# A power on GpSimd in place of a logarithm, an exponential and three corrections

## The chip, the cores and the metric

The kernel runs on one core of a Trainium2 chip. Five engines work side by side, each with a queue of its own that it executes in order: TensorE (PE, matmuls; its weight loads are shown as PEld), VectorE (DVE), ScalarE (ACT), GpSimd (POOL) and SyncE (SP, which here only issues transfers). The metric is the device time of one execution in microseconds (us); lower is better.

## The reference

The reference is one layer of a streaming encoder for 528 new frames of one stream (16 learned meta tokens and 512 prompt frames) and 64 further frames of a running stream with 128 cached ones. The model width is 2048.

```python
def rmsnorm(x, g):
    y = x * lax.rsqrt(jnp.mean(x * x, axis=-1, keepdims=True) + EPS)
    return y * g

h = rmsnorm(x, norm_attn_g)
z = h @ w_in                                  # q, k, v of 8 differential heads; latents of MLA
cq = rmsnorm(z[..., OFF_CQ:OFF_CKV], mla_q_norm_g);  qm = cq @ mla_w_uq
ckv = rmsnorm(z[..., OFF_CKV:OFF_KR], mla_kv_norm_g); km, vm = expand_latent(ckv, mla_w_ukv)
o_d, o_m = attention(...)                     # chunk-causal, both head groups
o_d = rmsnorm(o_d, diff_subln_g) * (1 - lam_init)     # one norm per head of 128 columns
x = x + concatenate([o_d, o_m]) @ w_out
h = rmsnorm(x, norm_ffn_g)
x = x + (silu(h @ w_gate) * (h @ w_up)) @ w_down      # inner width 5632
y = rmsnorm(x, final_norm_g)
```

Everything is float32. The new keys, values and latents are outputs too.

## The kernel before, in words

Activations are held transposed, features on the 128 partitions and tokens along the columns: T = 592 columns with the meta tokens, TQ = 576 without. Every weight and activation is split into a high and a low part (`wh`, `wl`; `xh`, `xl`): ScalarE writes the high part with a copy to a reduced format, VectorE subtracts it from the original, and TensorE multiplies high by high, high by low and low by high.

Because tokens run along the columns, the mean square of a token is a sum over partitions. A matmul with a matrix of ones gives that sum on all 128 partitions at once, so that the reciprocal square root of a norm is taken of a whole 128x576 or 128x592 tile in most places. `rsqrt(r, v)` does this: a logarithm (`Ln`) and an exponential of minus a half of it (`Exp`) on ScalarE, and then one correction step of Newton's method on VectorE, in three instructions, the last of which writes r. `v` is overwritten.

The places are these, in order of time:

- the norm before attention: squares are summed with tokens on the partitions, so `ss` and `rc` are 128x5 only; ten small matmuls (`prb`) then spread `rc` over the columns as `rb`, with which the projections' results are scaled (`z`)
- `diff_attend`, once for each of the eight differential heads: the head's output `o32` (name `o` in the profile), its squares `sq`, the sum `pq`, the mean square written back to `sq` by VectorE, `rsqrt(r, sq)`, and the scaling of `o32` by `g08` and `r`. The outputs of heads 0 to 6 are stored to DRAM (`mspill`) and loaded back for the output projection; head 7's is split into `mxh` and `mxl` at once
- `key_latent_norm` (`v`, `r`, then `zl` scaled), whose results are transposed for an output and serve as keys and values of the second head group
- `query_norm` (`v`, `rsq`): `rsq` multiplies the projected queries of the second head group (`zq`, `zn`)
- `token_norm` before the FFN (`sq2` and `rb2`, shown as `sq` and `rb`): `rb2` multiplies the gate's sums `c` before and after SiLU, in `gated`
- `token_rows`, the last stage, with tokens on the partitions again: four groups of 128 tokens and one of 64, with a mean square of 128x1 or 64x1 each. Groups 0 to 3 call `rsqrt`. The last group has a written-out form of it, in which the logarithm takes its sum and bias itself while VectorE writes `v`.

TensorE's instructions run in the order in which the program lists them. A small model of time (`Streams`) decides in what order the generators for projections, heads and norms are advanced while the program is written, and so how matmuls of different stages interleave. VectorE's, ScalarE's and SyncE's instructions keep their written order only in the first stage, in the stretch from the last head to the start of the FFN, and where `pin` is used; elsewhere the order of their queues is set by the program builder from written order, dependencies and its own estimates of durations. GpSimd's queue is always ordered in that second way. GpSimd otherwise holds some fills (`bias`, `p`), additions of squares, parts of the rotary embedding, and in the FFN the sums of weight blocks (`ws`) and products of `c`.

The attention stage uses a PSUM bank pair `sp` (one buffer) for scores; VectorE's instruction `e<-sp,bias` adds the bias and frees it. The pair `ps` (two buffers) takes projections. Weights of the projections have two buffers each for `wh` and `wl`.

In the last stage ScalarE's table set with logarithm and exponential is loaded again by a pinned `preload_act_table_set`; SiLU in the FFN uses another set.

Of the kernel before, what the change touches and what calls it, by code (L numbers as in the profile page):

```python
# [11 lines left out]
F32 = mybir.dt.float32  # L12
F32R = mybir.dt.float32r
AF = mybir.ActivationFunctionType
ALU = mybir.AluOpType
# [4 lines left out]
P = 128  # L20
D = 2048
# [110 lines left out]
def encoder_step(  # L132
# [8 lines left out]
    V, S, Q, G = Engine(tc, nc.vector), Engine(tc, nc.scalar), Engine(tc, nc.sync), nc.gpsimd  # L141
# [3 lines left out]
    cp = ctx.enter_context(tc.tile_pool(name="cp", bufs=1))  # L145
# [7 lines left out]
    def store(dst, src):  # L153
        Q.dma_start(dst, src)
# [3 lines left out]
    def f32(ap):  # L158
        return ap.bitcast(F32)
# [8 lines left out]
    def split_scaled(hi, lo, src, g):  # L168
        S.activation(hi, src, AF.Copy, scale=g)
        V.scalar_tensor_tensor(lo, src, g, f32(hi), op0=ALU.mult, op1=ALU.subtract)  # L170

    def rsqrt(r, v):

        S.activation(r, v, AF.Ln)
        S.activation(r, r, AF.Exp, scale=-0.5)
        V.tensor_tensor(v, v, r, op=ALU.mult)
        V.scalar_tensor_tensor(v, v, -0.5, r, op0=ALU.mult, op1=ALU.mult)
        V.scalar_tensor_tensor(r, v, 1.5, r, op0=ALU.add, op1=ALU.mult)

    def weights(src, kcs, cols, pool=None):  # L180
        pool = pool or wp
# [179 lines left out]
    with ExitStack() as ph:  # L361
# [25 lines left out]
        x = {}  # L387
# [942 lines left out]
    def pin(ins):  # L1330
        if pinned[0]:
            tc.keep_in_program_order(ins)
# [37 lines left out]
    def pmt():  # L1370
        return pm.tile([P, 512], F32, name="m", tag="m")
# [117 lines left out]
    for i in range(KC):  # L1489
        x = ma.tile([P, TQ], F32, name="x", tag="x", bufs=3)  # L1490
# [352 lines left out]
    def column(i, o, n):  # L1843
        if i in columns:
            return columns[i][:, o:o + n]
        return y5[0][:, o:o + n] if o + n <= 384 else y5[1][:, o - QH:o - QH + n]

    def token_rows(g, d):

        o, n = groups[g]  # L1850
        q, last = d // 2, g == len(groups) - 1
        fine = last and d > 5
        if d % 2 == 0 or fine:
            banks0[g, q] = pmt()
        bank = banks0[g, q][0:n, :]
        c0 = d % 2 * 256
        for k, (hi, lo) in enumerate(acts):
            wh, wl = kept[d][k]
            for i, (a, b) in enumerate(((hi, wh), (hi, wl), (lo, wh))):
                PE.matmul(bank[:, c0:c0 + 256], a[:, o:o + n], b, start=k + i == 0,  # L1860
                          stop=k == len(acts) - 1 and i == 2)
        for f in range(2):
            c = c0 + f * P
            PE.matmul(bank[:, c:c + P], column(2 * d + f, o, n), ident, start=False, stop=True,  # L1864
                      is_transpose=True, skip_group_check=True)
        ss = small[0:n, 8 * g:8 * g + 8]
        v, b, r = (small[0:n, a + g:a + g + 1] for a in (40, 48, 56))
        cs = slice(c0, c0 + 256) if fine else slice(0, 512)
        if d % 2 or fine:
            at = q + (last and d == 7)  # L1870
            S.activation(junk[0:n, cs], bank[:, cs], AF.Square, accum_out=ss[:, at:at + 1])
            if last and d < 7:
                V.tensor_tensor(whole[0:n, 512 * q + cs.start:512 * q + cs.stop], bank[:, cs], gain[q][0:n, cs],
                                op=ALU.mult)
        if last and d == 6:
            V.tensor_reduce(b, ss[:, 0:4], axis=AX.X, op=ALU.add)
            V.tensor_scalar(b, b, 1.0 / D, EPS, op0=ALU.mult, op1=ALU.add)
        elif last and d == 7:
            x = ss[:, 4:5]
            S.activation(r, x, AF.Ln, bias=b, scale=1.0 / D)  # L1880
            V.scalar_tensor_tensor(v, x, 1.0 / D, b, op0=ALU.mult, op1=ALU.add)
            S.activation(r, r, AF.Exp, scale=-0.5)
            V.tensor_tensor(v, v, r, op=ALU.mult)
            V.scalar_tensor_tensor(v, v, -0.5, r, op0=ALU.mult, op1=ALU.mult)
            V.scalar_tensor_tensor(r, v, 1.5, r, op0=ALU.add, op1=ALU.mult)
            w = whole[0:n, :]
            V.scalar_tensor_tensor(w[:, 1792:2048], bank[:, cs], r, gain[3][0:n, cs], op0=ALU.mult, op1=ALU.mult)
            S.activation(w[:, 0:512], w[:, 0:512], AF.Copy, scale=r)
            V.tensor_scalar(w[:, 1024:1792], w[:, 1024:1792], r, None, op0=ALU.mult)
            store(y_sample[:, 1024:2048], w[:, 1024:2048])  # L1890
            S.activation(w[:, 512:1024], w[:, 512:1024], AF.Copy, scale=r)
            S.dma_start(y_sample[:, 0:1024], w[:, 0:1024])
        elif d == 7:
            V.tensor_reduce(v, ss[:, 0:4], axis=AX.X, op=ALU.add)
            V.tensor_scalar(v, v, 1.0 / D, EPS, op0=ALU.mult, op1=ALU.add)
            rsqrt(r, v)
            for q in range(4):
                ot = room(names)[0:n, 0:512]
                V.scalar_tensor_tensor(ot, banks0.pop((g, q))[0:n, :], r, gain[q][0:n], op0=ALU.mult, op1=ALU.mult)
                store(y_prompt[o:o + n, q * 512:(q + 1) * 512], ot)  # L1900
# [18 lines left out]
    for bi, n in enumerate(blocks):  # L1919
        slots = [(first + k) % 8 for k in range(n)]  # L1920
        if bi + 1 < len(blocks):
            if bi + 2 == len(blocks):
                build = builder(first + n, blocks[bi + 1])
            else:
                build = fetcher(first + n, 4)

            def step():
                next(start, None)
                next(build, None)
                next(keeping, None)  # L1930
                next(late, None)

            keeping, late = iter(()), iter(())
            if bi + 2 == len(blocks):
                rest = [m for m in range(8) if m not in slots]
                free = [f"b{p}_{m}" for m in rest[::-1][:2] for p in ORDER]
                free += [f"b{p}_{m}" for m in rest[:-2] for p in (3, 6, 7)]
                free += [f"b{p}_{m}" for m in slots for p in ORDER]
                names = iter(free)
                fifth_raws, fifth_weights = (itertools.cycle([next(names) for _ in range(2)]) for _ in range(2))  # L1940
            for d in range(KC // 2):
                if bi + 2 == len(blocks) and d == 2:
                    keeping = plain_weights(first + n)
                if bi + 2 == len(blocks) and d == 4:
                    S.activation(y5[0][:, QH:384], y5[1][:, 0:384 - QH], AF.Copy)
                if bi + 3 == len(blocks) and d == KC // 2 - 1:
                    late = late_parts(first + n + 4)
                if bi == 0 and d == 1:
                    accumulator(4, y234[:, 2 * TQ:3 * TQ])
                    y5 = [None, y234[:, 3 * TQ:3 * TQ + QH]]  # L1950
                    load(y5[1], x2spill[5, :, QH:TQ])
                    fetch_raw(first, n, 3)
                elif bi == 0 and d == 2:
                    Q.ordered = False
                    close_fb()
                    yy, close_yy = pool("yy")
                    y5[0] = yy.tile([P, 384], F32, name="y5")
                    y[5] = [y5[0][:, 0:QH], y5[1]]
                    load(y[5][0], x2spill[5, :, 0:QH])
                if bi == 0 and 2 < d < KC // 2 - 1:  # L1960
                    fetch_raw(first, n, d + 1)
                if bi == 0 and d > 1:
                    for i in range(2 * d + 2, min(2 * d + 4, KC)):
                        accumulator(i, yy.tile([P, TQ], F32, name=f"y{i}"))
                if (first, d) not in fetched:
                    fetch_raw(first, n, d)
                down_rows(first, n, d, slots, step)
            for g in (build, keeping, late):
                for _ in g:
                    pass  # L1970
        else:
            pin(S.preload_act_table_set("natural_log_exp_and_others"))

            small, junk = room(names), room(names)[:, 0:512]
            whole = fr.tile([P, 2048], F32, name="whole", tag="raw", bufs=2)
            gain = [room(names)[:, 0:512] for _ in range(4)]
            for q in range(4):
                load(gain[q], g_fin[q * 512:(q + 1) * 512].unsqueeze(0).to_broadcast([P, 512]))
            for g in range(5):
                for d in range(KC // 2):  # L1980
                    token_rows(g, d)
        first += n
# [78 lines left out]
```

## Time and profile before

| what | value |
|---|---|
| median of 3 runs | 2387.84 us (2387.77 to 2390.52) |
| span of the profiled execution | 2389.4 us |
| profiled execution against the median | 1.6 us above it, inside the runs' range |
| TensorE busy | 2361.4 us (99%) |
| VectorE busy | 1794.6 us (75%) |
| ScalarE busy | 1161.9 us (49%) |
| GpSimd busy | 705.5 us (30%) |
| first projections and first norm | 0 to 65 us |
| projections and differential heads | 65 to 520 us |
| latent heads and output projection | 520 to 790 us, its second part and the first FFN weights to 935 us |
| gate and up projections | to about 1860 us |
| down projection | to about 2343 us |
| last block, final norm and outputs | to 2389.4 us |

The profile's span runs from the first to the last instruction of the profiled execution; no time around it is listed. In lines of the timeline the first number is the start in us from the beginning of the span, the second the length in us, then engine, line, operation, the tile written and the tiles read, and in brackets how long the engine had been idle before and for what. Most instructions of VectorE, ScalarE and SyncE go through one helper and so have line L125; they are told apart by their tiles. In lines that group instructions, an x with a number is their count.

### The profile page before, as it was taken

What the parts mean: (1) busy time and instruction counts of PE and PEld (TensorE: products, weight loads), DVE (VectorE), ACT (ScalarE), POOL (GpSimd) and SP (SyncE); (2) the same over time, 40 slices, a digit from 0 to 9 for tenths busy, and PEclk for the clock granted to TensorE, in tenths of its full rate; (3) what the DMA queues carried; (4) which work ended last, traced back from release to release, by engine and by line L of the source; (5) the groups of instructions that cost most, each with busy time, mean ns of one, the idle gap of its engine ahead of it and who ended that gap; (6) DMA issues with size and microseconds to landing.
All of it is one profiled execution on the core that took longest, in us unless ns stands there. A gap on an engine that the chain in (4) does not pass through costs nothing.

```text
span 2389.4 us, 44637 instructions
## 1 busy us (share of the span) xinstructions
PE 2361.4 (99%) x17558; PEld 2330.0 (98%) x17558; DVE 1794.6 (75%) x2878; ACT 1161.9 (49%) x2262; POOL 705.5 (30%) x553
## 2 busy tenths in 40 slices
PE   9999999999999999999999999999999999999998
PEld 8999999999999999999999999999999999999998
DVE  5665656776555788788888888888888888888984
ACT  5544445455444554445545555545545433333444
POOL 0000000020001345554454454554554322222320
PEclk9999999999999999999999999999999999999999
DMA  9423333353223553334434434434434975645432
GB/s 277 125 85 86 93 87 94 94 157 116 89 94 107 168 176 108 120 112 151 154 118 151 155 116 151 163 110 155 160 113 153 324 260 170 227 161 169 159 102 98
DMA packets 330547, 340.93 MB, mean 143 GB/s; under 512 B 22610, under 2 KB 272376, under 8 KB 330304
## 3 DMA queue, kind: packets, MB, share of 16 engines
q1 hardware_dynamic: 328720, 334.30, 43.1%
q0 software_dynamic: 1104, 3.22, 0.4%
q8 instruction: 138, 2.26, 0.4%
q10 hardware_dynamic: 512, 0.55, 0.1%
q14 instruction: 73, 0.60, 0.1%
HBM read 267.21 MB, written 74.15 MB: 143 GB/s over the span
## 4 chain that ended last, share of the span: by engine, by line
PE 58%; DVE 1%; DMA 1%; issue 0%; POOL 0%; ACT 0%; DVEq 0%; POOLq 0%; SPq 0%; ACTq 0%
PE m L1454 38%; PE m L1458 19%; PE m L1860 1%; DVE wl L125 1%; DMA raw<-in_ffn_w_down 1%; PE m L1864 0%; DVE ws L125 0%; DMA b<-sumspill 0%; POOL ws L1414 0%; DVE y L125 0%; ACT b L125 0%; DVE b L125 0%; DVE whole L125 0%; DVE c L125 0%; ACT whole L125 0%
## 5 line engine op out<-in xcount | busy, mean ns | idle before, releaser
L1454 PE MATMUL m<-b,wh 128*128 128x288 f32 x7168 | 1052.5, 296 | 4.1 <-DVE y L125 2.7
L1454 PEld LDWEIGHTS m<-b,wh 128*128 128x128 f32 x7168 | 984.0, 189 | 6.7 <-ACT wh L125 4.2
L1458 PE MATMUL m<-b,wl 128*128 128x288 f32 x3584 | 569.8, 295 | 2.0 <-DVE wl L125 1.9
L1414 POOL TENSOR_TENSOR ws<-raw 128x512 f32<-128x512 f32 (+1 forms) x258 | 366.7, 1430 | 542.0 <-DVE wl L125 237.8
L1458 PEld LDWEIGHTS m<-b,wl 128*128 128x128 f32 x3584 | 509.2, 189 | 3.5 <-DVE wl L125 3.4
L125 ACT ACTIVATE wh<-ws 128x512 fp32r<-128x512 f32 (+1 forms) x339 | 282.9, 845 | 393.9 <-PE m L1454 244.4
L125 DVE TENSOR_TENSOR wl<-ws,wh 128x512 fp32r<-128x512 f32 (+1 forms) x339 | 386.8, 1149 | 98.5 <-ACT wh L125 93.0
L125 DVE TENSOR_TENSOR wl<-raw,wh 128x512 fp32r<-128x512 f32 (+1 forms) x393 | 367.8, 959 | 13.5 <-ACT wh L125 11.1
L125 ACT ACTIVATE wh<-raw 128x512 fp32r<-128x512 f32 (+1 forms) x393 | 230.9, 620 | 291.8 <-PE m L1454 241.6
L108 PE MATMUL ps<-xh,wh 128*128 128x296 f32 (+1 forms) x960 | 217.6, 308 | 1.7 <-ACT wh L125 1.7
L108 PE MATMUL ps<-xl,wh 128*128 128x296 f32 (+1 forms) x960 | 208.4, 298 | 0.0
L108 PE MATMUL ps<-xh,wl 128*128 128x296 f32 (+1 forms) x928 | 202.1, 299 | 0.5 <-DVE wl L125 0.5
L125 DVE TENSOR_TENSOR y<-y,m 128x288 f32<-128x288 f32 x280 | 125.4, 449 | 57.7 <-PE m L1458 56.3
L108 PEld LDWEIGHTS ps<-xh,wh 128*128 128x128 f32 x960 | 155.5, 190 | 5.5 <-ACT wh L125 2.1
L125 DVE TENSOR_TENSOR ws<-ws,raw 128x512 f32<-128x512 f32 (+1 forms) x129 | 111.7, 870 | 60.8 <-POOL ws L1414 58.5
L108 PEld LDWEIGHTS ps<-xl,wh 128*128 128x128 f32 x960 | 155.6, 189 | 0.3 <-DVE xl L125 0.2
L108 PEld LDWEIGHTS ps<-xh,wl 128*128 128x128 f32 x928 | 151.1, 189 | 1.0 <-DVE wl L125 1.0
L125 DVE TENSOR_TENSOR wl<-wr,wh 128x1024 fp32r<-128x1024 f32 (+1 forms) x106 | 111.2, 1050 | 29.8 <-ACT wh L125 28.4
L125 ACT ACTIVATE wh<-wr 128x1024 fp32r<-128x1024 f32 (+1 forms) x108 | 97.3, 903 | 59.2 <-PE ps L108 36.2
L1679 POOL TENSOR_TENSOR c<-c,rb 128x576 f32<-128x576 f32 x42 | 67.1, 1599 | 168.7 <-ACT c L125 168.7
L703 POOL MEMSET bias<- 64x64 f32 x8 | 1.2, 144 | 365.1 <-DMA bias<-tsk 311.6
L125 ACT ACTIVATE parts<-c 128x1 fp32r<-128x1 f32 (+1 forms) x266 | 85.7, 322 | 32.3 <-DVE c L125 26.3
(427 smaller groups left out, 3139.2 us busy)
## 6 DMA issues: line engine op xcount, KB each, us to landing
raw<-in_ffn_w_gate SPq DMA_DIRECT2D x44, 1024.0 KB, 5.9
raw<-in_ffn_w_up SPq DMA_DIRECT2D x44, 1024.0 KB, 6.5
raw<-in_ffn_w_down SPq DMA_DIRECT2D x39, 1024.0 KB, 5.5
partspill<-parts SPq DMA_DIRECT2D x133, 288.0 KB, 2.1
b<-partspill SPq DMA_DIRECT2D x133, 288.0 KB, 6.2
wr<-in_w_in SPq DMA_DIRECT2D x54, 512.0 KB, 3.8
wr<-in_w_out SPq DMA_DIRECT2D x16, 512.0 KB, 4.0
wr<-in_w_out SPq DMA_DIRECT2D x24, 256.0 KB, 3.0
```

The costliest lines, as they stand in the source:

```text
L108: self.tc.keep_in_program_order(self.pe.matmul(out, lhsT, rhs, start=start, stop=stop))
L125: ins = issue(*args, **kwargs)
L703: G.memset(bias[0:64, 464:528], -BIG)
L1414: engine.tensor_tensor(w[:, k:k + m, :], pick(xs), pick(ys), op=op)
L1454: PE.matmul(banks[p], wh[k], x, start=first and new and k == 0 and x is hi, stop=False, skip_group_check=not new)
L1458: PE.matmul(banks[p], wl[k], hi, start=False, stop=last and k == n - 1, skip_group_check=not new)
L1679: engine.tensor_tensor(g[:, f, :], g[:, f, :], rb2, op=ALU.mult)
L1860: PE.matmul(bank[:, c0:c0 + 256], a[:, o:o + n], b, start=k + i == 0, stop=k == len(acts) - 1 and i == 2)
```

## The change

`rsqrt` becomes one instruction on GpSimd, `r = v ** -0.5`, an elementwise power with a 128x1 tile of -0.5 spread over the columns as its second operand. That tile is filled once by VectorE at the start. All places call it; the last group of the last stage loses its written-out form and calls `rsqrt` after VectorE has written `v`. The second load of the table set with logarithm and exponential is removed.

```diff
+    minus_half = cp.tile([P, 1], F32, name="minus_half")
+    V.memset(minus_half, -0.5)
+
     def rsqrt(r, v):
-
-        S.activation(r, v, AF.Ln)
-        S.activation(r, r, AF.Exp, scale=-0.5)
-        V.tensor_tensor(v, v, r, op=ALU.mult)
-        V.scalar_tensor_tensor(v, v, -0.5, r, op0=ALU.mult, op1=ALU.mult)
-        V.scalar_tensor_tensor(r, v, 1.5, r, op0=ALU.add, op1=ALU.mult)
+        G.tensor_tensor(r, v, minus_half[0:v.shape[0]].to_broadcast(list(v.shape)), op=ALU.pow)
...
             x = ss[:, 4:5]
-            S.activation(r, x, AF.Ln, bias=b, scale=1.0 / D)
             V.scalar_tensor_tensor(v, x, 1.0 / D, b, op0=ALU.mult, op1=ALU.add)
-            S.activation(r, r, AF.Exp, scale=-0.5)
-            V.tensor_tensor(v, v, r, op=ALU.mult)
-            V.scalar_tensor_tensor(v, v, -0.5, r, op0=ALU.mult, op1=ALU.mult)
-            V.scalar_tensor_tensor(r, v, 1.5, r, op0=ALU.add, op1=ALU.mult)
+            rsqrt(r, v)
...
-            pin(S.preload_act_table_set("natural_log_exp_and_others"))
```

## The prediction

> **What bounds the kernel now.** I read the page first, its busy shares, slices and chain, then the groups of instructions on GpSimd, then the timeline around each norm.
>
> ```profile
> PE 2361.4 (99%) x17558; PEld 2330.0 (98%) x17558; DVE 1794.6 (75%) x2878; ACT 1161.9 (49%) x2262; POOL 705.5 (30%) x553
> PE 58%; DVE 1%; DMA 1%; issue 0%; POOL 0%; ACT 0%; DVEq 0%; POOLq 0%; SPq 0%; ACTq 0%
> ```
>
> The span is 2389.4 us, so TensorE is idle for 28.0 us of it, and the chain that ends last is matmuls with a per cent each of VectorE and DMA. ScalarE and VectorE work is worth nothing by itself here; it counts where it makes a matmul wait. Matmuls stand in a fixed order, so a wait is lost for good. The profiled span is 1.6 us above the median of the runs, 2387.84; I add the differences to the median. A change of 0.2% is 4.8 us, about what a measurement of this kernel can tell from none.
>
> **What is removed.** Seventeen places compute a reciprocal square root. Eleven are wide, with 576 or 592 columns (eight heads, the key latents, the query latents, the tokens before the FFN); the others are the 128x5 of the first norm, four 128x1 and the tail's 64x1. The head norms show what goes at a wide place:
>
> ```profile
> L125 ACT ACTIVATE r<-sq x8: 684/685/688, 138.5 to 509.2; 128x576 f32<-128x576 f32 x8
> L125 ACT ACTIVATE r<-r x9: 684/686/699, 139.2 to 509.9; 128x576 f32<-128x576 f32 x8, 128x592 f32<-128x592 f32 x1
> L125 DVE TENSOR_TENSOR sq<-sq,r x8: 757/759/1394, 139.9 to 510.7; 128x576 f32<-128x576 f32 x8
> L125 DVE SCALAR_TENSOR_TENSOR sq<-sq,r x8: 748/759/760, 140.7 to 512.7; 128x576 f32<-128x576 f32 x8
> L125 DVE SCALAR_TENSOR_TENSOR r<-sq,r x8: 747/758/759, 141.5 to 513.4; 128x576 f32<-128x576 f32 x8
> ```
>
> Two activations of 0.69 and three corrections of 0.76 are 3.7 us of work, about 40 us over eleven places. It lies beside matmuls and gives TensorE nothing. What matters is when the result comes.
>
> **What is added: one power per place, with no row of its own.** The nearest rows on GpSimd:
>
> ```profile
> L1796 POOL TENSOR_TENSOR c<-c 128x576 f32<-128x576 f32 x42 | 73.5, 1749 | 86.0 <-DVE c L125 82.1 <-issue 3.7
> L635 POOL MEMSET q00z<- 64x576 f32 x1 | 0.6, 583 | 50.8 <-DMA xspill<-xt 50.8
> L1414 POOL TENSOR_TENSOR ws<-b 128x128 f32<-128x128 f32 x16 | 9.8, 610 | 2.3 <-DMA b<-in_ffn_w_down 2.3
> L1353 POOL TENSOR_TENSOR b<-b 128x288 f32<-128x288 f32 x4 | 3.2, 808 | 28.5 <-ACT b L125 28.5
> ```
>
> A product of two 128x576 tiles takes 1.75 us; a pass without input takes 0.58. A power is a logarithm, a product and an exponential; ScalarE's tables do the first and last in a pass, and GpSimd shows no such pass. I count some 14 multiply-adds for the two series. Lower bound: they hide behind the reading, X = 1.75 us. Upper: each costs a full two-input pass, 15 x 1.75 = 26 us. I take each at the input-free pass, 14 x 0.58 + 1.75 = 9.9, so X = 10 us (an estimate), nearest to the memset row since a step needs no new operand. For 64x1 the two narrow rows give (808 - 610)/160 = 1.24 ns a column and so 0.45 us at none; I take 0.4, between 0 and 1.
>
> The Trainium skill's page GPSIMD Engine Reference, section on elementwise cycle accounting, says a loop body of three or more operations runs at about 3 operations a cycle at 1.2 GHz. By it 14 steps on 576 columns would be an estimated 2.2 us and the change would cost nothing (the third rival). No run here shows it.
>
> **Heads 0 to 6.** The first, on the timeline:
>
> ```profile
> 137.62 0.75 DVE L125 TENSOR_SCALAR sq<-pq 128x576 f32<-128x576 f32 x1
> 142.28 0.82 DVE L125 SCALAR_TENSOR_TENSOR o<-o,gT,r 128x576 f32<-128x576 f32 x1
> 143.19 0.77 DVE L125 TENSOR_TENSOR z<-ps,rb 128x592 f32<-128x592 f32 x1
> 146.06 0.29 DVE L125 CUSTOM_DVE_ANT_0 e<-sp,bias 128x144 f32<-128x144 f32 x1
> 147.06 0.37 PE L108 MATMUL sp<-kh,q10s 128*128 128x272 f32 x1
> ```
>
> The mean square is ready at 138.37 and the scaling of the head's output begins at 142.28. The scaling's own result is not urgent: it is stored, and read back long after. But VectorE works its queue in order, and if the scaling keeps its place, z and the score evacuation e stand behind it, and the next scores need the bank that e frees. With 0.1 us of handoff the power ends at 138.47 + 10 = 148.47; the scaling is 6.2 us late, e with it. e ended at 146.35 and the matmul began at 147.06: 0.7 us of slack. Lost: 5.5 us, generally X - 4.5. For seven heads 38.5 us. On GpSimd's queue the power has the next head's bias memset behind it, some 23 us later here, so it delays nothing there below X of about 20.
>
> **Head 7**, whose output goes straight to matmuls:
>
> ```profile
> 508.37 0.76 DVE L125 TENSOR_SCALAR sq<-pq 128x576 f32<-128x576 f32 x1
> 513.54 3.93 POOL L1009 TENSOR_TENSOR rkl<-kr,rkh 64x592 fp32r<-64x592 f32 x2 [2.11 <-ACT rkh L125]
> 514.23 1.92 DVE L125 SCALAR_TENSOR_TENSOR o<-o,gT,r 128x576 f32<-128x576 f32 x1
> 519.09 0.74 DVE L125 TENSOR_TENSOR mxl<-o,mxh 128x576 fp32r<-128x576 f32 x1
> 519.77 0.40 PE L108 MATMUL pso<-mxh,wh 128*128 128x288 f32 x1
> ```
>
> Power 509.23 to 519.23, scaling 0.82, the split's two halves 0.69 and 0.74, 0.2 between: 521.7 instead of 519.83, 1.9 us lost (X - 8.1). The scaling took 1.92 here beside GpSimd's 3.93 and 0.82 alone: the two engines slow each other. A power that computes more than it reads should do so less; I take 0, with 1.1 us for each VectorE instruction beside it as the other bound.
>
> **Key and query latents.**
>
> ```profile
> 450.10 0.77 DVE L125 TENSOR_SCALAR v<-sp 128x592 f32<-128x592 f32 x1
> 455.72 1.57 DVE L125 SCALAR_TENSOR_TENSOR zl<-zl,gT,r 128x592 f32<-128x592 f32 x2
> 458.22 0.38 PE L112 MATMUL pn<-ident,zl 128*128 128x128 f32 x2
> ...
> 528.94 0.45 DVE L125 TENSOR_SCALAR v<-pq 128x288 f32<-128x288 f32 x1
> 534.68 0.76 DVE L125 SCALAR_TENSOR_TENSOR zq<-ps,rsq 128x576 f32<-128x576 f32 x1
> 536.40 0.75 DVE L125 TENSOR_TENSOR xo<-xo,ps 128x576 f32<-128x576 f32 x1 [0.97 <-PE ps L108]
> 542.57 0.42 PE L108 MATMUL ps<-mxh,wh 128*128 128x288 f32 x2
> ```
>
> Keys: power to 460.97, two scalings to 462.6, transposes due at 458.22: 4.4 us lost (X - 5.6). Queries: power to 539.5, zq and xo to 541.1, bank due at 542.57: nothing lost (X - 11.5 above that).
>
> **Tokens before the FFN.**
>
> ```profile
> 913.34 0.81 DVE L125 TENSOR_SCALAR sq<-m 128x288 f32<-128x288 f32 x2
> 919.26 2.52 DVE L125 TENSOR_TENSOR c<-c,rb 128x576 f32<-128x576 f32 x2
> 919.42 3.51 POOL L1414 TENSOR_TENSOR ws<-raw 128x512 f32<-128x512 f32 x2 [13.55 <-DVE wl L125]
> 924.07 1.32 PE L1458 MATMUL m<-b,wl 128*128 128x288 f32 x8 [0.42 <-DVE wl L125]
> ```
>
> Power 914.25 to 924.25; the products of c start 5.0 us late, the low weight halves behind them too, and TensorE already waits for one: 5.0 us lost (X - 5). GpSimd's subtotals of 919.42, queued behind the power, are late by the same 5 us, inside that loss.
>
> **First norm and tail.**
>
> ```profile
> 59.73 0.17 DVE L125 TENSOR_SCALAR ss<-ss 128x5 f32<-128x5 f32 x1
> 60.81 0.17 DVE L125 SCALAR_TENSOR_TENSOR rc<-ss,rc 128x5 f32<-128x5 f32 x1
> 61.34 0.83 PE L108 MATMUL prb<-ident,rc 128*128 128x128 f32 x6
> ...
> 2337.33 1.28 ACT L125 ACT_TABLE_LOAD   x1
> 2381.80 0.15 DVE L125 SCALAR_TENSOR_TENSOR b<-b 64x1 f32<-64x1 f32 x1
> 2382.53 0.34 DVE L125 SCALAR_TENSOR_TENSOR b<-b 64x1 f32<-64x1 f32 x2
> ```
>
> First norm: ready at 59.90 + 0.1 + 0.4 = 60.4 instead of 60.98, the matmul busy elsewhere until 61.34: nothing. Tail: v at 2381.95, the power to 2382.45, instead of 2382.87: 0.4 us gained, and this is on the path to the end (0.8 gained to 0.2 lost). The four 128x1 places lie under matmuls of the following rows. The table load of 1.28 us leaves ScalarE among waits: nothing. The fill of minus_half stands before the first data.
>
> **Sum:** 38.5 + 1.9 + 4.4 + 0 + 5.0 - 0.4 = 49.4 us, 2387.84 + 49.4 = 2437 us. It rests on X and on the queue order.
>
> **Rivals.** *The steps run one behind the other (B).* At X = 26 the same terms are 7 x 21.5 + 17.9 + 20.4 + 14.5 + 21.0 - 0.4 = 224, giving 2612 us; for it, only that the engine's simplest wide product already takes 1.75 us where VectorE takes 0.76. The Trainium skill, same page, section on performance pitfalls, gives 4 cycles a step for a dependent chain: 14 steps would be an estimated 27 us; no run here shows it.
>
> *The queue order gives way (C).* VectorE's queue here is ordered by the program builder from its own estimates; with z, e and the FFN splits ahead of the scaling, only real readers wait: 1.9 + 4.4 - 0.4 = 5.9, 2394 us. Against it: the builder must hold the power for long.
>
> *Not slower (D).* Up to X = 4.5 the power ends no later than the old five instructions plus their slack, all terms vanish but the tail: 2387.4 us; at X = 5 it is 7 x 0.5 - 0.4 = 3.1, still within 0.2%. That X decides. For it: the lower bound of 1.75.
>
> *Faster (E).* VectorE, freed of 25 us, lets matmuls start that waited for it. It would have to end 4.8 of TensorE's 28 idle us: 2383 us. Against it: VectorE's share of the chain is 1%.
>
> **Chances:** forecast 0.36, B 0.16, C 0.09, D 0.34, E 0.05. Slower 0.61, same 0.34, faster 0.05. The forecast's own range is X of 6 to 15, 2399 to 2491 us. For 8 in 10 it goes down to 2386 (D whole) and up to X = 20, 108.5 + 11.9 + 14.4 + 8.5 + 15.0 - 0.4 = 158, 2546 us, leaving out E and most of B.
>
> **What would show it.** GpSimd's group of powers, eight of 128x576: its mean is X. Right: 7 to 13 us, VectorE's longest waits are of the scaling for r on GpSimd, and TensorE waits near the head norms and at 914 to 930. Wrong if X is below 5 (times as before, TensorE's idle time still 28), or if VectorE does other work between mean square and scaling. In the tail one GpSimd instruction should stand between v and the output, and the table load be gone.

## The result, and the profile after

The changed kernel takes 3386.39 us (median of 4 runs, 3384.77 to 3389.03), the kernel before 2387.81 us beside it (4 runs): a ratio of 1.417, with an interval of 1.415 to 1.419. It is slower, as forecast, but by 999 us where 49 were forecast. One price explains most of it. The page of the changed kernel begins:

```profile
span 3386.9 us, 44561 instructions
PE 2388.5 (71%) x17558; PEld 2353.7 (69%) x17558; DVE 1770.3 (52%) x2828; ACT 1143.7 (34%) x2227; POOL 1722.2 (51%) x570
PE   9723507154150062099995399999999999999999
PEclk9857758576675585599997699999999999999999
POOL 0376493855959948900047854445445554222231
```

GpSimd works 1722.2 us where it had 705.5. TensorE has holes in the first two fifths of the span, and in most of those slices GpSimd is busy instead and TensorE's granted clock is down. From the gate and up projections on, everything is as it was. The groups of GpSimd's instructions on `rsqrt`'s line (count, then busy time, mean ns of one) show why:

```profile
L176 POOL TENSOR_TENSOR r<-sq,minus_half 128x576 f32<-128x576 f32 x8 | 738.8, 92345 | 200.7 <-DVE sq L125 180.4 <-DMA cos<-c_cos 20.3
L176 POOL TENSOR_TENSOR r<-v,minus_half 128x592 f32<-128x592 f32 x1 | 94.8, 94757 | 7.5 <-DVE v L125 7.5
L176 POOL TENSOR_TENSOR rsq<-v,minus_half 128x576 f32<-128x576 f32 x1 | 92.2, 92194 | 2.8 <-DVE v L125 2.8
L176 POOL TENSOR_TENSOR rb<-sq,minus_half 128x576 f32<-128x576 f32 x1 | 92.6, 92601 | 8.4 <-DVE sq L125 8.4
```

One wide power takes 92.3 us, nine times the 10 us assumed and 3.5 times the 26 us of the upper bound. What TensorE waited for, from the view of the waits (us in total, times, longest):

```profile
PE pna L112 <- DVE z L125: 347.4, 4, 88.2
PE sp L108 <- DVE nm L125: 176.7, 5, 88.7
PE pn L112 <- DVE nn L125: 92.8, 1, 92.8
PE m L1452 <- ACT wh L125: 91.2, 2, 91.0
PE pn L112 <- DVE zl L125: 88.6, 2, 88.3
PE pso L108 <- ACT wh L125: 88.3, 1, 88.3
PE pso L108 <- DVE xo L125: 87.0, 1, 87.0
DVE o L125 <- POOL r L176: 738.4, 8, 92.4
```

Seven heads (4 + 2 + 1 long waits in the first three lines), the tokens before the FFN, the key latents, head 7, the query latents: eleven wide places, eleven waits of 85 to 93 us. (`pna` takes transposes of `z`; `nm` is written beside the scores' `e`; `nn` is a copy of transposed key latents. VectorE's `z`, `nm` and `nn` all stand behind a scaling in its queue.) None of these lines names GpSimd as what TensorE waited for; it is VectorE and ScalarE, and only VectorE's own wait, the last line, names the power. The first head on the timeline shows the chain:

```profile
137.72 0.75 DVE L125 TENSOR_SCALAR sq<-pq 128x576 f32<-128x576 f32 x1
138.61 92.22 POOL L176 TENSOR_TENSOR r<-sq,minus_half 128x576 f32<-128x576 f32 x1 [30.26 <-DVE sq L125]
...
230.87 0.82 DVE L125 SCALAR_TENSOR_TENSOR o<-o,gT,r 128x576 f32<-128x576 f32 x1 [92.39 <-POOL r L176]
231.60 0.77 DVE L125 TENSOR_TENSOR z<-ps,rb 128x592 f32<-128x592 f32 x1
...
232.43 1.11 PE L112 MATMUL pna<-ident,z 128*128 128x128 f32 x4 [85.42 <-DVE z L125]
```

The scaling of the head's output waits 92.39 us for r, though its own result goes only to DRAM; `z`, which does not need r, stands behind it in VectorE's queue and starts as soon as the scaling lets it; TensorE, out of work 85 us before, waits for `z`.

The sum closes. The seven lines of TensorE's waits make 972 us. TensorE is idle for 3386.9 - 2388.5 = 998.4 us, against 28.0 before: 970.4 more. It is also busy for 27.1 us more with the same 17,558 matmuls. Together 997.5, which is the difference of the spans (3386.9 - 2389.4). The 27 us come from the clock, in this table of windows around the end of the first wait (length; busy time of PE, PEld, DVE, ACT, POOL; granted clock; DMA share and GB/s):

```profile
228.00:232.40 4.40, 0.00 (x0) 0.00 (x0) 1.53 (x3) 0.00 (x0) 2.83 (x1) 0.50 0.00 0
...
236.40:238.40 2.00, 2.00 (x10) 2.00 (x9) 1.93 (x7) 0.12 (x1) 0.00 (x0) 0.50 0.06 17
238.40:240.40 2.00, 2.00 (x11) 1.94 (x10) 1.07 (x6) 1.16 (x5) 0.00 (x0) 0.54 0.47 131
240.40:242.40 2.00, 2.00 (x15) 2.00 (x14) 1.41 (x5) 0.54 (x1) 0.00 (x0) 1.00 0.08 21
```

After the wait the matmuls run at half clock until about 240, some 8 us after the first of them; ten instructions in 2 us, then fifteen. The Trainium skill's page TensorE: Matmul & The Clock Gate, Part 1, tells of two states, half clock after at least one idle window of about 3.4 us and full clock after a busy one. The trace agrees on the two states; the way back took longer here, with gaps in the first 4 us, and less idle time was enough for the fall. In the kernel before, a wait of 2.26 us ended at 1874.90, and the next 3.41 us are at half clock:

```profile
1871.76:1875.17 3.41, 1.15 (x9) 0.95 (x8) 3.41 (x8) 2.75 (x7) 1.08 (x1) 1.00 1.05 364
1875.17:1878.58 3.41, 3.41 (x16) 3.41 (x15) 2.54 (x6) 0.00 (x0) 1.70 (x3) 0.50 1.07 373
```

### The profile page after: what moved, and what is told of

It is laid out like the page before. It is cut to its first block, busy times and chain, and to the rows that moved or that the text cites. A ratio compares the mean times of both kernels' runs of the same rounds, so it can differ in the third digit from the quotient of the medians.

```text
span 3386.9 us, 44561 instructions
## 1 busy us (share of the span) xinstructions
PE 2388.5 (71%) x17558; PEld 2353.7 (69%) x17558; DVE 1770.3 (52%) x2828; ACT 1143.7 (34%) x2227; POOL 1722.2 (51%) x570
## 3 DMA queue, kind: packets, MB, share of 16 engines
q8 instruction: 138, 2.26, 0.3%
## 5 line engine op out<-in xcount | busy, mean ns | idle before, releaser
L176 POOL TENSOR_TENSOR r<-sq,minus_half 128x576 f32<-128x576 f32 x8 | 738.8, 92345 | 200.7 <-DVE sq L125 180.4
L125 DVE SCALAR_TENSOR_TENSOR o<-o,gT,r 128x576 f32<-128x576 f32 x8 | 7.7, 964 | 738.4 <-POOL r L176 738.4
L112 PE MATMUL pna<-ident,z 128*128 128x128 f32 x64 | 11.6, 313 | 347.4 <-DVE z L125 347.4
L112 PEld LDWEIGHTS pna<-ident,z 128*128 128x128 f32 x64 | 8.8, 159 | 348.4 <-DVE z L125 348.3
L125 ACT ACTIVATE kh<-z 64x592 fp32r<-64x592 f32 x32 | 22.3, 695 | 358.9 <-DVE z L125 358.5
```

Of the source, the lines that this page charges most:

```text
L112: self.tc.keep_in_program_order(self.pe.transpose(out, in_, identity))
L125: ins = issue(*args, **kwargs)
L176: G.tensor_tensor(r, v, minus_half[0:v.shape[0]].to_broadcast(list(v.shape)), op=ALU.pow)
```

## The experiments

Three groups of kernels ran on three occasions; the kernel before ran beside each, with medians of 2390.43 us (21 runs), 2390.04 (13) and 2389.92 (19), a little above the 2387.8 that the expectations use. Ratios are against the runs of the same group.

**Is it the power or the move?** A product in its place, so that queues, tiles and waits stay and only the operation differs. The power is left out.

```diff
-    V.memset(minus_half, -0.5)
+    V.memset(minus_half, 0.01)
-        G.tensor_tensor(r, v, minus_half[...].to_broadcast(...), op=ALU.pow)
+        G.tensor_tensor(r, v, minus_half[...].to_broadcast(...), op=ALU.mult)
```

> Left out: the power. The changed kernel with a product by 0.01 in its place on GpSimd, at all seventeen places; every wait, queue and order of the change stays, only the instruction is another. Theory (the price of the power, 92.2 us for 128x576, is the whole loss): the product takes about 1.6 us, less than the 4.5 us that the heads can bear, so 2387 us, within 3 us of the kernel before. Rival (moving the step to GpSimd's queue costs by itself, whatever it computes): most of the 1000 us stays, above 2600 us.

Measured: 2388.48 us (10 runs), ratio 0.9996 (0.9987 to 1.0005). The group of GpSimd's instructions at that line:

```profile
L176 POOL TENSOR_TENSOR r<-sq,minus_half 128x576 f32<-128x576 f32 x8 | 10.4, 1304 | 201.8 <-DVE sq L125 201.8
```

An operation of the same shape in the same place takes 1.3 us and costs nothing. So the whole loss comes with the power, and not with the move. It also shows that taking the activations and corrections off ScalarE and VectorE gains nothing that this can measure: VectorE is busy 1766.6 us instead of 1794.6, and the time is the same.

**Does the price go with the columns?** The power on the left half of the eleven wide places, the old five instructions (`newton`) on the rest.

```diff
     def rsqrt(r, v):
+        w = v.shape[1]
+        if w > 8:
+            newton(r[:, w // 2:w], v[:, w // 2:w])
+            r, v = r[:, 0:w // 2], v[:, 0:w // 2]
         G.tensor_tensor(r, v, minus_half[...].to_broadcast(...), op=ALU.pow)
```

> The power on the left half of the columns at the eleven wide places, the old five instructions on the right half. X should be 0.4 + 288 x 0.159 = 46.3 us, since the 128x5 power took 1.20 and the 128x576 one 92.18. Theory (VectorE waits in its queue, and the matmuls behind it, for X less a slack): 7 x (46.3 - 4.5) + 38.2 + 40.7 + 34.8 + 41.3 - 0.4 = 447 us, 2835 us, up to 25 us more where the clock sinks in the waits. Rival (GpSimd is simply too busy: a power per head has to fit the 53 us between heads): 46.3 fits, the heads lose nothing, and only head 7, the latents and the tokens cost their 155 us, 2543 us.

Measured: 2865.30 us (4 runs), ratio 1.199 (1.197 to 1.201).

```profile
L187 POOL TENSOR_TENSOR r<-sq,minus_half 128x288 f32<-128x288 f32 x8 | 370.2, 46272 | 200.2 <-DVE sq L125 200.2
```

46.3 us is half of 92.3, and the loss is halved too, with the waits (TensorE's eleven long ones are of 37.6 to 44.0 us) and 24.6 us of slower matmuls on top: the price goes by the columns, and the loss goes by the latency at each place.

**Only the narrow places.** The power at 128x5, 128x1 and 64x1, the old five at the wide ones.

```diff
     def rsqrt(r, v):
+        if v.shape[1] > 8:
+            return newton(r, v)
         G.tensor_tensor(r, v, minus_half[...].to_broadcast(...), op=ALU.pow)
```

> The power only where it is narrow (128x5, four 128x1, the tail's 64x1), the old five instructions at the eleven wide places; no second load of the table set. Theory (price by columns): the narrow ones take 0.5 to 1.2 us; the tail ends 0.4 us earlier as in the changed kernel, 2387.4 us, 0.4 us faster than before. Rival (each power has a fixed price on the engine that the first norm and the tail feel): 2389 us or more.

Measured: 2389.16 us (11 runs), ratio 0.9995 (0.9987 to 1.0004). The narrow places cost nothing. In the tail the timeline of this kernel shows

```profile
2380.96 0.19 ACT L125 ACTIVATION_READ_ACCUMULATOR b<-m 64x1 f32 x1
2381.18 0.15 DVE L125 SCALAR_TENSOR_TENSOR b<-b 64x1 f32<-64x1 f32 x1 [0.19 <-ACT b L125]
2381.41 0.54 POOL L185 TENSOR_TENSOR b<-b,minus_half 64x1 f32<-64x1 f32 x1 [6.29 <-DVE b L125]
2381.99 1.33 ACT L125 ACTIVATE whole<-whole,b 64x512 f32<-64x512 f32 x2 [0.84 <-POOL b L185]
```

From the end of the sum, 2381.15, to the output, 2381.99, are 0.84 us; before, it was 1.24. The 0.4 us are there in the trace and far below what the times can tell.

**The price by itself.** The kernel before, with nine powers of several widths, partitions, exponents and bases and one product more on GpSimd, in the first 40 us, while it has nothing to do. Nothing reads their results.

```diff
+            G.tensor_tensor(res[0:P, 0:64], lab[0:P, 0:64], lab[0:P, 96:97].to_broadcast([P, 64]), op=ALU.pow)
...
+            G.tensor_tensor(res[0:16, 96:112], lab[0:16, 0:16], lab[0:16, 96:97].to_broadcast([16, 16]), op=ALU.pow)
...
+            G.tensor_tensor(res[0:P, 192:208], lab[0:P, 0:16], lab[0:P, 98:99].to_broadcast([P, 16]), op=ALU.mult)
```

> The kernel before, with eleven extra instructions on GpSimd in its idle first 50 us, whose results nobody reads: powers of 128x64, 128x16, 64x16 and 16x16 with the exponent -0.5, of 128x16 with 0.5, 2 and 1, of the bases 1 and 0.01, and one product. Theory (a loop over columns, the same work for each): 10.6 us for 64 columns, 2.9 us for each 16, whatever the exponent and the base; 16 and 64 partitions as long as 128, if each column is done for all partitions at once. Rival (element by element within a group of partitions): with 16 partitions the same, since each of eight groups of 16 has a processor of its own. Rival (a general routine with short cuts for easy operands): exponents 1 and 2 or the base 1 take well under half. The product about 0.3 us. The time of the kernel 2388 us.

Measured: 2390.36 us in one run, and on the timeline, in the order of the code: base 1.37 with exponent -0.5 on 128x64; then on 128x16, 64x16 and 16x16; four rows of 2.88, 2.88, 2.89 and 2.89 us on 128x16, with exponents 0.5, 2 and 1 and with base 1, left out here; base 0.01; the product.

```profile
5.39 10.57 POOL L422 TENSOR_TENSOR res<-lab 128x64 f32<-128x64 f32 x1
15.93 2.89 POOL L423 TENSOR_TENSOR res<-lab 128x16 f32<-128x16 f32 x1
18.79 2.89 POOL L424 TENSOR_TENSOR res<-lab 64x16 f32<-64x16 f32 x1
21.65 2.88 POOL L425 TENSOR_TENSOR res<-lab 16x16 f32<-16x16 f32 x1
...
35.95 2.96 POOL L430 TENSOR_TENSOR res<-lab 128x16 f32<-128x16 f32 x1
38.88 0.39 POOL L431 TENSOR_TENSOR res<-lab 128x16 f32<-128x16 f32 x1
```

(10.57 - 2.89) / 48 = 0.160 us a column, and 0.33 us at none. That gives 92.5 us for 576 columns, where 92.3 were measured. Neither the partitions, nor the exponent, nor the base matter much (2.88 to 2.96): there is no short cut for a square, for a first power or for a base of one. That 16 partitions take as long as 128 fits the theory and the first rival alike; this does not tell them apart.

**The forecast's own condition.** The power on 60 columns at every wide place, so that its time is what the prediction had assumed, X = 9.9 us.

```diff
...
+        if w > 8:
+            newton(r[:, 60:w], v[:, 60:w])
+            r, v = r[:, 0:60], v[:, 0:60]
```

> The power on 60 columns at all eleven wide places, the old five instructions on the rest: X = 0.33 + 60 x 0.160 = 9.9 us, the price that the prediction assumed. Theory (the prediction's sum is right for its X): 7 x 5.4 + 1.8 + 4.3 + 0 + 4.9 - 0.4 = 48 us, 2436 us, and up to 25 us more if the clock sinks after these short waits too. Rival (short waits are taken up by idle time of VectorE behind them): under 2415 us.

Measured: 2458.44 us (4 runs), ratio 1.029 (1.027 to 1.032), or 68 us more. The power took 10.0 us. The line of the page, and below it the three largest totals among TensorE's waits (us in total, times, longest):

```profile
PE 2386.5 (97%) x17558; PEld 2352.6 (96%) x17558; DVE 1790.5 (73%) x2861; ACT 1157.2 (47%) x2249; POOL 819.7 (33%) x570
```

```profile
PE sp L108 <- DVE nm L125: 24.0, 6, 5.0
PE m L1467 <- DVE wl L125: 5.8, 3, 4.9
PE pso L108 <- ACT wh L125: 4.9, 1, 4.9
```

The waits are of 2.8 to 5.0 us at ten of the eleven places, none at the query latents, as the prediction's terms have it. TensorE is idle for 45.4 us more than before (73.4 instead of 28.0), and the terms sum to 48. That is partly luck: the seven heads lost 32 us instead of 38, head 7 lost 4.9 instead of 1.8. On top, the matmuls take 25.1 us more (2386.5 - 2361.4). So short a wait is enough to lose the clock. The windows around the first one, where TensorE is idle for 3.11 us until 150.12 and, a little later, for 1.61 until 152.38:

```profile
148.00:150.00 2.00, 0.00 (x0) 0.00 (x0) 1.44 (x3) 0.00 (x0) 0.52 (x1) 1.00 0.00 0
150.00:152.00 2.00, 0.66 (x4) 0.42 (x4) 2.00 (x4) 1.87 (x3) 0.00 (x0) 0.91 0.39 147
...
156.00:158.00 2.00, 2.00 (x10) 1.94 (x10) 1.07 (x6) 1.25 (x5) 0.00 (x0) 0.50 0.47 131
158.00:160.00 2.00, 2.00 (x14) 2.00 (x13) 1.21 (x4) 0.25 (x1) 0.00 (x0) 0.89 0.08 21
```

So even at the assumed X the forecast's 49 us would have been 68: the terms for the waits were about right in sum, though not each, and a term for the clock was missing.

**Where it turns.** The same with 24 columns, X = 4.2 us, below the 4.5 from which the prediction lets heads lose anything.

```diff
...
+            newton(r[:, 24:w], v[:, 24:w])
+            r, v = r[:, 0:24], v[:, 0:24]
```

> The power on 24 columns at all eleven wide places, the old five instructions on the rest: X = 0.33 + 24 x 0.160 = 4.2 us. Theory (up to X = 4.5 the slack holds): 2387.4 us, within 3. Rival (any wait of VectorE for GpSimd costs): 2395 us or more.

Measured: 2393.78 us (10 runs), ratio 1.0019 (1.0009 to 1.0029): 4.5 us, more than expected, less than the rival had it, and little beside 68. TensorE's busy time is 2361.1, as before, and no wait of it is longer than 1.8 us, so the slack covers most of a power of 4.2 us. TensorE is idle for 30.9 us in the profiled run, against 28.0; where the rest of the 4.5 us lies is not shown.

**Is it the result that is late, or the queue?** Heads 0 to 6 need their scaled output only much later. First the power on 192 columns in these seven heads alone (31 us), with the scaling on VectorE as in the change:

```diff
+            if h < H - 1:
+                w = 192
...
+                    newton(r[:, w:TQ], sq[:, w:TQ])
+                G.tensor_tensor(r[:, 0:w], sq[:, 0:w], minus_half.to_broadcast([P, w]), op=ALU.pow)
...
```

> The power on 192 of 576 columns in heads 0 to 6 alone, the old five instructions for their other columns and at the four other wide places; the scaling stays on VectorE. X = 0.33 + 192 x 0.160 = 31.1 us by the bench. Theory (VectorE's queue stands behind the scaling): 7 x (31.1 - 4.5) = 186 us of waits, 7 x 2.5 us for matmuls at a sunken clock after each wait, 0.4 back in the tail: 2591 us. Rival (GpSimd's capacity): 31.1 us fit between heads 53 us apart, 2388 us.

Measured: 2588.24 us (4 runs), ratio 1.084 (1.082 to 1.086), as the blocked queue gives. Then the scaling on GpSimd too, behind the power, so that VectorE has nothing to wait for:

```diff
+                G.tensor_tensor(o32, o32, r, op=ALU.mult)
+                G.tensor_tensor(o32, o32, g08.to_broadcast([P, TQ]), op=ALU.mult)
-            V.scalar_tensor_tensor(o32, o32, g08, r, op0=ALU.mult, op1=ALU.mult)
```

> As the kernel with 192 columns in heads 0 to 6, but the scaling of those heads' outputs too is done on GpSimd, as two products behind the power, so that nothing on VectorE or ScalarE waits for the power; the store waits instead. Theory (the queue, not the result, makes the matmuls wait): 31.1 + about 3 us on GpSimd hide between heads, 2388 us within 5. Rival (the result itself is needed soon): as with the scaling on VectorE, 2591 us.

Measured: 2540.28 us (4 runs), ratio 1.064 (1.062 to 1.066). My expectation failed here: 48 us came back, not 200. The timeline shows what had been overlooked, with SyncE's queue of transfers (SPq) beside ScalarE and TensorE:

```profile
136.19 0.37 SPq L125 DMA_DIRECT2D wr<-in_w_in  x1
170.63 0.34 SPq L125 DMA_DIRECT2D mspill<-o  x1
171.07 0.37 SPq L125 DMA_DIRECT2D wr<-in_w_in  x1
...
175.57 1.06 ACT L125 ACTIVATE wh<-wr 128x1024 fp32r<-128x1024 f32 x1 [17.22 <-DMA wr<-in_w_in]
176.66 1.23 DVE L125 TENSOR_TENSOR wl<-wr,wh 128x1024 fp32r<-128x1024 f32 x1 [17.37 <-ACT wh L125]
...
180.29 0.44 PE L112 MATMUL pnb<-ident,z 128*80 128x128 f32 x1 [16.32 <-DVE na L125]
```

The store of the scaled head waits for GpSimd at the head of SyncE's queue, 34 us without a transfer; the next weights stand behind it, ScalarE waits for them 17 us, VectorE for ScalarE's `wh`, and TensorE for `na`, which stands behind `wl` in VectorE's queue. The waiting had only moved from one queue to another. So in the next kernel the store is issued from GpSimd's own queue, right behind the products:

```diff
-                store(mspill[h], o32)
+                G.dma_start(mspill[h], o32)
```

> The kernel with the power on 192 columns and the two products on GpSimd in heads 0 to 6, with one edit: the store of the scaled head is issued from GpSimd's own DMA queue, right behind the products, and no longer from SyncE's. In that kernel SyncE stood 244.9 us in 7 waits for GpSimd's o, with weight loads, bias loads and stores queued behind. Theory (nobody needs the result soon; what costs is the blocked in-order queue, SyncE's there): with nothing on VectorE, ScalarE or SyncE waiting for the power, 2540 comes down by over 100 us. What can still wait is GpSimd's own queue: the fill of the next head's bias, done at 161.8 in the kernel before, stands behind power and products, which end at 170.6, some 9 us later, and the loads of bias5 on SyncE stand behind that fill. If slack covers that: 2388 to 2395; if none of it is covered: 6 x 9 = 54, up to 2445. Rival (the power's lateness or its work on GpSimd itself costs, whichever queue holds the store): stays at 2500 or above.

Measured: 2391.42 us (10 runs), ratio 1.0008 (0.9998 to 1.0017). 149 us are gone by one line, with GpSimd's work unchanged:

```profile
139.06 30.95 POOL L769 TENSOR_TENSOR r<-sq,minus_half 128x192 f32<-128x192 f32 x1 [30.96 <-DVE sq L125]
170.08 1.43 POOL L770 TENSOR_TENSOR o<-o,r 128x576 f32<-128x576 f32 x1
171.58 1.15 POOL L771 TENSOR_TENSOR o<-o,gT 128x576 f32<-128x576 f32 x1
173.03 0.65 POOL L776 DMA_DIRECT2D mspill<-o  x1 [0.30 <-POOL o L771]
173.68 0.17 POOL L710 MEMSET bias<- 64x64 f32 x1
```

The result is no earlier (the products end at 172.73), GpSimd is busy for 954.4 us where it had 705.5 before the change, and nobody loses by it. The fill of the next head's bias comes at 173.68 instead of 161.76, and that costs nothing either. Last, this fill on VectorE:

```diff
-            G.memset(bias[0:64, 464:528], -BIG)
+            V.memset(bias[0:64, 464:528], -BIG)
```

> As the kernel with the store on GpSimd's own DMA queue, and the small fill of the next head's bias (64x64, 0.15 us) on VectorE, so that no engine but GpSimd waits for GpSimd in the heads. Theory: all waits for the power are gone, 2386 to 2393, the time of before within what a measurement can tell, although GpSimd still works 7 x 33.5 = 235 us more than before. If the kernel without this edit is already there, both are equal; if that one shows 2395 to 2445, the difference is the price of the fill behind the power. Rival (GpSimd's work or its share of a port slows the others, or the fill on VectorE blocks that queue in turn): above 2400.

Measured: 2392.43 us (10 runs), ratio 1.0004 (0.9994 to 1.0015), the same within the measurement: the fill behind the power had been hidden already.

No version here is measurably faster than the kernel before. The whole power in the heads would not fit in this way, though no run tried it: it takes 92 us, and in the profile before one head follows the other in some 53 us, (509.2 - 138.5) / 7 from the first and last start in the first row of the prediction's head norms.

## Why the prediction was wrong

**The step that failed** is the price: "I take each at the input-free pass, 14 x 0.58 + 1.75 = 9.9, so X = 10 us". Measured: 92.3. The way of building it failed, not only the number. Both bounds treated a power as 15 passes at most, at the rate of GpSimd's fills and products; the count of 14 had no row, and no run shows it. In the runs a power costs 0.160 us a column with every base and exponent tried. A product of the same shape in the same place took 1.3 us, a seventieth. The row of the memset to which the estimate was tied said nothing about that; no row of the trace before did, and an upper end of 26 us from products was no bound at all, since nothing in those rows excludes that a power is 70 products. The two estimates by the Trainium skill's page GPSIMD Engine Reference, 2.2 us by about three operations a cycle and 27 us by four cycles a step, missed it as well; whether its rules do not hold for this instruction or the 14 steps were too few is not shown. With the clock of 1.2 GHz that the same page of the Trainium skill states, 0.160 us would be 192 cycles a column, an estimate.

**The terms with the measured price.** The prediction's formula, with X = 92.2 (94.8 for the key latents), beside TensorE's longest wait at each place:

| place | by the prediction's terms | measured |
|---|---|---|
| heads 0 to 6 | 7 x (X - 4.5) = 613.9 | 85.4 + 86.9 + 88.7 + 86.2 + 86.9 + 88.2 + 92.8 = 615.1 |
| key latents | X - 5.6 = 89.2 | 88.3 |
| head 7 | X - 8.1 = 84.1 | 88.3 |
| tokens before the FFN | X - 5 = 87.2 | 91.0 |
| query latents | X - 11.5 = 80.7 | 87.0 |
| slower matmuls | none | 27.1 |
| tail | -0.4 | -0.4 |

The sum by the terms is 954.7, by the right column 996.4. So of the 949 us between forecast and result, 905 are X (954.7 - 49.4) and 42 are other steps; two or three are not in the table.

- *Heads 0 to 6*: right, mechanism and size; in four of the seven, TensorE waited for `z` itself before it came to the scores. VectorE's queue kept the scaling in its place, so the rival of the queue that gives way fell.
- *Query latents*, "bank due at 542.57: nothing lost (X - 11.5 above that)": the slack was wrong. In the changed program TensorE ran out 6.9 us after the mean square (1345.81 to 1352.70), not 13.2. It waited there for the `xo` that stands behind the scaling; this `xo` read the pair `ps` before and reads `pso` now. The blocks of matmuls had moved against the norm, and a slack read off the old order doesn't hold for the new one.
- *Head 7*: 4.2 us more lost. TensorE ran out 8.9 us after the mean square, not 10.7, and the matmul came 4.4 us after the power, not 2.5. The scaling took 1.98 us beside GpSimd's next product `kr`, where 0.82 were assumed, and the last to come was not the head's split but ScalarE's high weight half `wh`, behind that split in ScalarE's queue.
- *Tokens before the FFN*: 3.8 us more lost. TensorE ran out 4.2 us after the mean square, where a matmul had been due 9.9 us after it. It started again 2.5 us after the power, where 4.8 had been reckoned: here too it waited for `wh`, behind the product `c` in ScalarE's queue, and not for the low halves. That ScalarE stands in both chains was not followed.
- *The clock* had no term. "Lost: 5.5 us" counted the wait and not the half clock behind it. At X = 9.9 this alone was 25 of 68 us.
- *First norm and tail*: right. The 128x5 power took 1.20 us where 0.4 were assumed, and ended at 61.24; the small matmuls began at 61.40, at 61.34 before. The tail's power took 0.54 us, and the output started 0.84 us after the sum instead of 1.24.
- *ScalarE and VectorE relieved*: right that it is worth nothing; the kernel with the product in place of the power shows it, and with it the rival "faster" falls.
- *Not slower (D)*: its turning point near X = 4.5 to 5 is only bracketed, with 4.5 us lost at X = 4.2 and 68 at X = 10; its condition, so short a power, was far off.
- *GpSimd's queue*, "delays nothing there below X of about 20": too cautious; with 34 us in front of it, the fill of the bias still cost nothing.

## What to carry over

Where an operation has no row in the trace, other operations of the same engine and shape give no upper end of its price: here the power was 70 times the product. Price a new producer by its latency in front of every in-order queue that holds a reader, and count that queue's next urgent instruction, not the reader's own urgency; a lazy reader in a busy queue is an urgent one, and moving the reader only helps if the next in the chain, down to the store's queue, is moved too. A wait of TensorE of a few us costs more than its length, since the matmuls behind it run at half clock for some us.

## What the runs showed of the hardware

- An elementwise power on GpSimd: 0.33 us and 0.160 us a column, from 16 to 128 partitions and with all exponents and bases tried; 92.3 us for 128x576, 10.0 for 128x60.
- TensorE's granted clock fell to 0.50 at all ten places with waits of 2.8 to 5.0 us, and in the kernel before after one of 2.26 us; after one of 2.27 us in the kernel with the store on GpSimd's queue it did not fall. Behind the eleven waits of the changed kernel it was back at 1.00 3.1 to 8.5 us after the first matmul.
- Matmuls took 2.2 to 2.5 us longer for each long wait, whether the waits were of 88 us (27.1 us for 11 places), 42 (24.6 for 11), 26 (17.1 for 7) or 3 to 5 (25.1 for 10). With the scaling on GpSimd and the store on SyncE it was about 1 us for each (6.7 for 7), in part because fewer matmuls ran at half clock. Matmuls were busy at 0.50 for 64.9 us in the changed kernel, for 28.5 there and for 10.2 in the kernel before; half of the difference is an estimate of the loss, 27 and 9 us.
- GpSimd busy for 249 us more slowed neither VectorE nor TensorE measurably, as long as nobody waited for it. In that kernel VectorE's `wl` of 128x1024, between 60 and 520 us, took 1.225 us beside a power and 1.226 otherwise (medians).
